# A mixture-of-experts stage put into a hand-written order on every engine

## The chip, the cores and the metric

The kernel runs on one core of a Trainium2 chip. The metric is the device time of one execution in microseconds (us). A core has a matrix engine (TensorE, PE in the rows; PEld is its loading of stationary operands), a vector engine (VectorE, DVE), a scalar engine (ScalarE, ACT), a general engine (GpSimd, POOL) and a queue that issues transfers (SyncE, SP). Each engine works through its own instructions in a fixed order and waits at semaphores for the others.

## The reference, cut to what matters

One transformer block for 256 tokens of width 2048, all in fp32: attention and a gated recurrence, then a hierarchical mixture of experts, on which the change works. A router gives every token one of 4 groups and two of its 8 experts. Cut to the experts:

```python
y = jnp.zeros_like(h)
for gi in range(N_GROUPS):                       # 4 groups of 8 experts
    cg = jnp.where(grp == gi, comb, 0.0)         # weights of the token's two experts
    lo, hi = gi * EXPERTS_PER_GROUP, (gi + 1) * EXPERTS_PER_GROUP
    a = jnp.einsum('bsd,edf->bsef', h, w_gate[lo:hi])
    u = jnp.einsum('bsd,edf->bsef', h, w_up[lo:hi])
    y = y + jnp.einsum('bsef,efd->bsd', jax.nn.silu(a) * u * cg[..., None], w_down[lo:hi])
x = x + gt2[:, None] * y
return rmsnorm(x, g_final)
```

Each of the 32 experts has three matrices of 2048 x 512, 12 MB in fp32; all 32 are read once.

## The kernel before, in words

A framework traces the program and assigns buffers and semaphores; a planner in it, with a cost model of its own, then picks the order in which the instructions of each engine are issued. The order of the text is a starting point that the planner may leave.

The dense stages (input products, attention, recurrence, output product) come first; `route` works out for each token its place among the tokens of each expert (`self.pos`, at most 64 places, `CAP`). Then `experts` (line 1130) goes over the experts in groups of 2, 2 and then seven times 4 (`GATHERS`), and in each group over pairs of experts:

- **Places and gather.** Two matrices of zeros and ones `P` (line 1149, DVE) say which token sits at which place of the group's experts. `gather` (lines 1269 to 1283) multiplies the normalized tokens, held as two rounded halves, by `P`: for each of 16 slices of 128 columns four matmuls (line 1278) into one PSUM bank and one ACTIVATE (line 1281) that writes the slice `xg[j]`. A group's 16 slices are needed by all of its experts; `xg` has 18 buffers.
- **Gate and up.** An expert is worked off in four blocks `u`. A block has two loads of 1 MB (`slot`, lines 1119 to 1125, issued by SP) and multiplies four slices by both (line 1167: 8 fp32 products, which are 16 matmul instructions); gate goes to PSUM partitions 0 to 63, up to 64 to 127.
- **Hidden.** DVE copies the accumulators (line 1170), PE transposes them (line 1173), ACT applies silu (line 1176), DVE multiplies (line 1178).
- **Weights of the places.** For each pair DVE builds weighted places `Pc` (line 1184), PE transposes them (line 1186); from this come the scatter matrix `sc` (line 1188) and a column of token weights `cw` (line 1191).
- **Down and scatter.** Four chunks of 512 columns per pair. Each has two loads of 1 MB, 16 matmul instructions for both experts (line 1201), a scaling by DVE (line 1204), and a split into two rounded halves, the first by ACT (line 1206), the second by DVE (line 1207). `scatter` (lines 1285 to 1294) multiplies both halves by `sc` (four matmuls, line 1291) and DVE adds the two results to the tokens (line 1292). In the text a chunk's scatter stands after the next chunk's split (`waiting`); the planner may place it elsewhere.

All loads of the stage are issued by SP in one queue. Their buffers are a ring of 12 slots of 1 MB in a fixed rotation (`ring_order`: four of "ring", one of "t8", seven of "ring2"), so a load is issued when the matmuls that last read its slot are done. A pair takes 24 loads, the stage 384. PSUM has 4 banks for accumulators (`acc`) and 3 for gather, transposes and scatter (`misc`). Before the last pair's down chunks `prepare_finish` (lines 1305 to 1316) takes two slots of "ring" for the output and restarts the rotation with the two that are left and "ring2". `overflow` runs only if an expert has more than 64 tokens, `finish` scales the result and writes it.

Of the kernel before, what the change touches and what calls it, by code (L numbers as in the profile page):

```python
# [10 lines left out]
OP = mybir.AluOpType  # L11
# [124 lines left out]
class Block:  # L136
# [993 lines left out]
    def experts(self):  # L1130
        self.sec = "moe"
        nc, a = self.nc, self.a
        V = nc.vector
        mm = nc.tensor.matmul
# [3 lines left out]
        gt2 = self.gt2  # L1138
        iota = self.k[:, K_IOTA:K_IOTA + CAP]
        wg, wu, wd = a["w_exp_gate"], a["w_exp_up"], a["w_exp_down"]  # L1140
        waiting = None
        for g4, ge in enumerate(GATHERS):
            first = sum(GATHERS[:g4])
            P = []
            for t in range(2):
                p = self.mt([128, ge, CAP], "P", 4, F32R)
                for i in range(ge):
                    e = first + i
                    V.tensor_scalar(p[:, i, :], iota, self.pos[:, t, e:e + 1], None, op0=OP.is_equal)
                P.append(p.rearrange("p e s -> p (e s)"))  # L1150
            xg = []
            if g4:
                self.gather(P, xg, KT)
            for pr in range(ge // 2):
                e0 = first + 2 * pr
                gT = []
                for i in range(2):
                    e = e0 + i
                    sl = slice((2 * pr + i) * CAP, (2 * pr + i + 1) * CAP)
                    gu = self.acc()  # L1160
                    for u in range(4):
                        wgu = [self.slot(w[e, u], [128, 4, FF]) for w in (wg, wu)]
                        self.gather(P, xg, 4 * u + 4)
                        for jj in range(4):
                            j = 4 * u + jj
                            for k in range(2):
                                mm(gu[64 * k:64 * k + 64, :], xg[j][:, sl], wgu[k][:, jj, :], start=j == 0, stop=j == KT - 1,  # L1167
                                   skip_group_check=True)
                    gs = self.mt([128, FF], "gu", 2)
                    V.tensor_copy(gs, gu)  # L1170
                    ps = self.misc()
                    for f in range(4):
                        nc.tensor.transpose(ps[:, f * 128:(f + 1) * 128], gs[:, f * 128:(f + 1) * 128], self.ident)  # L1173
                    v = ps.rearrange("p (f s) -> p f s", f=4)
                    si = self.mt([128, 4, CAP], "si", 2)
                    nc.scalar.activation(si, v[:, :, 0:CAP], AF.Silu)  # L1176
                    h = self.mt([128, 4, CAP], "hT", 4)
                    V.tensor_mul(h, si, v[:, :, CAP:2 * CAP])
                    gT.append(h)
                ps = self.misc()  # L1180
                for t in range(2):
                    p = self.mt([128, 2, CAP], "Pc", 4)
                    for i in range(2):
                        V.tensor_scalar(p[:, i, :], iota, self.pos[:, t, e0 + i:e0 + i + 1], self.comb[:, t, e0 + i:e0 + i + 1],
                                        op0=OP.is_equal, op1=OP.mult)
                    nc.tensor.transpose(ps[:, t * 128:(t + 1) * 128], p.rearrange("p e s -> p (e s)"), self.ident)
                sc = self.mt([128, 256], "S", 2, F32R)
                V.tensor_scalar(sc, ps[:, 0:256], 0.0, None, op0=OP.is_gt)
                scr = self.mt([128, 256], "Sw", 2)
                cw = self.mt([128, 1], "cw", 2)  # L1190
                nc.scalar.activation(scr, ps[:, 0:256], AF.Copy, accum_out=cw)
                if e0 == N_EXP - 2:
                    self.prepare_finish()
                last = e0 == N_EXP - 2
                for c0, n in LAST_CHUNKS if last else DOWN_CHUNKS:
                    s = slice(c0, c0 + n)
                    wdd = [self.slot(wd[e0 + i, c0 // 512, :, :, c0 % 512:c0 % 512 + n], [128, 4, n]) for i in range(2)]
                    yp = self.acc()
                    for f in range(4):
                        for i in range(2):  # L1200
                            mm(yp[64 * i:64 * i + 64, :n], gT[i][:, f, :], wdd[i][:, f, :], start=f == 0, stop=f == 3,  # L1201
                               skip_group_check=True)
                    raw = self.mt([128, n], "ys", 2)
                    V.scalar_tensor_tensor(raw, yp[:, :n], cw, gt2[:, s], op0=OP.mult, op1=OP.mult)  # L1204
                    ys = [self.mt([128, n], "yp", 4, F32R) for _ in range(2)]
                    nc.scalar.activation(ys[0], raw, AF.Copy)  # L1206
                    V.tensor_sub(ys[1], raw, ys[0].bitcast(F32))
# [3 lines left out]
                if last:  # L1211
                    self.scatter(*waiting)
# [157 lines left out]
```

## Time and profile before

| | before |
|---|---|
| three runs, median (lowest to highest) | 1863.23 us (1863.08 to 1867.92) |
| the profiled execution, and its span from the first to the last instruction | 1862.79 us, 1861.0 us |
| PE busy | 1699.1 us (91% of the span) |
| DVE, ACT busy | 908.2 us (49%), 507.0 us (27%) |
| bytes moved | 630.38 MB, mean 339 GB/s |
| experts' stage, from the first gate matmul to the last instruction | 858.9 to 1861.0 us |

The profile is one execution. The busy time of an engine is the union of its instructions; a PE matmul's end is modelled, so a stretch of matmuls is best read from the start of the first to the start of what follows. The chain of work that ended last, which the profile follows back from the last instruction, ends here within the closing normalization and says nothing about the experts; where the stage is held up has to be read from the waits, the timeline and the stretches.

### The profile page before, as it was taken

Reading aid. Unit: us, or ns where it says so; the run is one execution under the profiler, and the core shown is the slowest. Engines: PE = TensorE matmul, PEld = TensorE weight load, DVE = VectorE, ACT = ScalarE, POOL = GpSimd, SP = SyncE. Lnnn points to the kernel's source line nnn. Section 1 sums busy time; section 2 is a strip of 40 time slices with the busy share of each in tenths; the row PEclk is TensorE's granted clock in tenths of the full one; section 3 lists DMA queues with packets and bytes.
Section 4 is the critical chain, followed back from the end, with each engine's and each line's share of the span. In section 5 each row is a group of like instructions: output and inputs, shape, how many; then the busy total and the mean of one; then the engine's idle time right before and its main releaser. Section 6 shows DMA issues by size and latency. Waiting matters only on the chain. (4 is left out here: it accounts for less than half of the span.)

```text
span 1861.0 us, 20334 instructions
## 1 busy us (share of the span) xinstructions
PE 1699.1 (91%) x7925; PEld 960.1 (52%) x7925; DVE 908.2 (49%) x1636; ACT 507.0 (27%) x845; POOL 17.3 (1%) x36
## 2 busy tenths in 40 slices
PE   6899999999999999997999888898898889988995
PEld 4566676777778878874434343342342423423322
DVE  3677589698788899854221232222212322122124
ACT  3333354555454434433202020020010200201112
POOL 0000000000000000000000000000000000000000
PEclk9999999999999999997999999999999999999998
DMA  7887745776668988868999999999999999999975
GB/s 283 285 292 287 280 163 194 260 290 262 226 246 309 355 310 329 331 226 323 396 400 378 422 421 408 421 394 421 421 393 421 392 422 421 393 420 422 394 311 227
DMA packets 96484, 630.38 MB, mean 339 GB/s; under 512 B 14864, under 2 KB 17216, under 8 KB 22016
## 3 DMA queue, kind: packets, MB, share of 16 engines
q1 hardware_dynamic: 95008, 626.01, 84.6%
q0 software_dynamic: 1200, 2.96, 0.6%
q8 instruction: 64, 1.05, 0.2%
q14 instruction: 36, 0.29, 0.0%
q10 hardware_dynamic: 176, 0.07, 0.0%
HBM read 626.90 MB, written 2.10 MB: 338 GB/s over the span
## 5 line engine op out<-in xcount | busy, mean ns | idle before, releaser
L1167 PE MATMUL moe_acc<-moe_u,moe_xg 128*64 128x512 f32 x2048 | 465.4, 596 | 0.0
L1167 PEld LDWEIGHTS moe_acc<-moe_u,moe_xg 128*64 128x64 f32 x2048 | 148.8, 137 | 285.7 <-issue 280.1
L1201 PE MATMUL moe_acc<-moe_u,moe_hT 128*64 128x512 f32 (+1 forms) x1040 | 261.4, 610 | 0.6 <-DMA moe_u<-w_exp_down 0.6
L1170 DVE COPY moe_gu<-moe_acc 128x512 f32<-128x512 f32 x32 | 22.1, 691 | 409.5 <-PE moe_acc L1167 409.5
L1291 PE MATMUL moe_ps<-moe_yp,moe_S 128*128 128x512 f32 (+1 forms) x260 | 92.5, 440 | 77.1 <-ACT moe_yp L1206 70.0
L1201 PEld LDWEIGHTS moe_acc<-moe_u,moe_hT 128*64 128x64 f32 x1040 | 76.2, 140 | 140.2 <-issue 137.0
L1176 ACT ACTIVATE moe_si<-moe_ps 128x256 f32<-128x256 f32 x32 | 12.3, 384 | 451.8 <-PE moe_ps L1173 451.8
L1204 DVE SCALAR_TENSOR_TENSOR moe_ys<-moe_acc,moe_cw,out_t 128x512 f32<-128x512 f32 (+1 forms) x65 | 48.2, 742 | 171.4 <-PE moe_acc L1201 171.4
L1206 ACT ACTIVATE moe_yp<-moe_ys 128x512 fp32r<-128x512 f32 (+1 forms) x65 | 40.4, 622 | 313.0 <-DVE moe_ys L1204 313.0
L1291 PEld LDWEIGHTS moe_ps<-moe_yp,moe_S 128*128 128x128 f32 x260 | 38.9, 188 | 142.8 <-ACT moe_yp L1206 111.4
L276 PE MATMUL gate_acc<-gate_wr,first_t 128*128 128x512 f32 x256 | 103.3, 404 | 0.0
L277 PE MATMUL gate_acc<-gate_wl,first_t 128*128 128x512 f32 x256 | 102.2, 399 | 0.0
L278 PE MATMUL gate_acc<-gate_wr,first_t 128*128 128x512 f32 x256 | 101.8, 397 | 0.0
L1292 DVE TENSOR_TENSOR out_t<-out_t,moe_ps 128x512 f32<-128x512 f32 (+1 forms) x130 | 83.6, 675 | 31.8 <-PE moe_ps L1291 31.8
L254 ACT ACTIVATE gate_wr<-gate_u 128x1024 fp32r<-128x1024 f32 x64 | 67.8, 1060 | 85.9 <-PE gate_acc L278 80.7
L1281 ACT ACTIVATE moe_xg<-moe_ps,pre_c,pre_c 128x256 f32<-128x256 f32 (+1 forms) x144 | 69.7, 541 | 73.9 <-PE moe_ps L1278 73.8
L255 DVE TENSOR_TENSOR gate_wl<-gate_u,gate_wr 128x1024 fp32r<-128x1024 f32 x64 | 78.0, 1222 | 23.1 <-ACT gate_wr L254 22.7
L1278 PEld LDWEIGHTS moe_ps<-moe_P,out_t 128*128 128x128 f32 x576 | 73.0, 195 | 22.5 <-issue 9.6
L1278 PE MATMUL moe_ps<-moe_P,out_t 128*128 128x256 f32 (+1 forms) x576 | 79.1, 289 | 4.1 <-DVE out_t L1292 3.4
L276 PE MATMUL lb_acc<-lb_wr,first_t 128*128 128x512 f32 (+1 forms) x208 | 78.8, 383 | 3.0 <-ACT first_t L523 2.4
L277 PE MATMUL lb_acc<-lb_wl,first_t 128*128 128x512 f32 (+1 forms) x208 | 78.7, 378 | 2.7 <-DVE lb_wl L255 2.7
L278 PE MATMUL lb_acc<-lb_wr,first_t 128*128 128x512 f32 (+1 forms) x208 | 78.0, 377 | 0.0
(436 smaller groups left out, 2506.5 us busy)
## 6 DMA issues: line engine op xcount, KB each, us to landing
moe_u<-w_exp_gate SPq DMA_DIRECT2D x128, 1024.0 KB, 11.4
moe_u<-w_exp_up SPq DMA_DIRECT2D x128, 1024.0 KB, 13.1
moe_u<-w_exp_down SPq DMA_DIRECT2D x126, 1024.0 KB, 12.3
gate_u<-w_in SPq DMA_DIRECT2D x32, 1024.0 KB, 4.8
gate_u<-w_ada SPq DMA_DIRECT2D x26, 1024.0 KB, 5.7
lb_u<-w_in SPq DMA_DIRECT2D x20, 1024.0 KB, 6.3
first_u<-w_ada SPq DMA_DIRECT2D x17, 1024.0 KB, 5.9
out_u<-w_out SPq DMA_DIRECT2D x16, 1024.0 KB, 6.5
```

The lines of the kernel that those rows point to most:

```text
L254: nc.scalar.activation(hi, raw, AF.Copy)
L255: nc.vector.tensor_sub(lo, raw, hi.bitcast(F32))
L276: mm(out, lr, hi, start=start, stop=False)
L277: mm(out, lr, lo, start=False, stop=False)
L278: mm(out, ll, hi, start=False, stop=stop)
L1167: mm(gu[64 * k:64 * k + 64, :], xg[j][:, sl], wgu[k][:, jj, :], start=j == 0, stop=j == KT - 1, skip_group_check=True)
L1201: mm(yp[64 * i:64 * i + 64, :n], gT[i][:, f, :], wdd[i][:, f, :], start=f == 0, stop=f == 3, skip_group_check=True)
L1204: V.scalar_tensor_tensor(raw, yp[:, :n], cw, gt2[:, s], op0=OP.mult, op1=OP.mult)
L1278: nc.tensor.matmul(ps[:, 0:n], self.xs[t][i][:, j * 128:(j + 1) * 128], P[t], start=t == 0 and i == 0, stop=t == 1 and i == 1)
L1281: nc.scalar.activation(x, ps[:, 0:n], AF.Identity, scale=self.mod["sc2"][:, j:j + 1], bias=self.mod["sh2"][:, j:j + 1])
L1291: self.nc.tensor.matmul(ps[:, :n], sc[:, t * 128:(t + 1) * 128], ys[i], start=i == 0, stop=i == 1)
L1292: self.nc.vector.tensor_add(self.z[t][:, s], self.z[t][:, s], ps[:, :n])
```

## The change

`experts` is rewritten inside `tc.manual_schedule()`: there each engine issues its instructions in the order of the text. That order is new: the first block of the next pair stands before the down chunks; a chunk is scattered after the next chunk's down matmuls, and the last chunk of a pair after block 1 of the next pair; the places of the next group are built, and its gather is issued four slices at a time, between the blocks of the group's last expert; the transposes of an expert's first member stand after the first block of its second. What is computed stays, and so do the loads, tile sizes, buffers and ring. The removed loop is printed above; "..." stands for removed lines, and blank lines are left out.

```diff
@@ -1128,90 +1128,150 @@
         return self.moe.tile(shape, dt, name=self.name(tag), tag=tag, bufs=bufs)
     def experts(self):
         self.sec = "moe"
         nc, a = self.nc, self.a
...
         self.ring_i = 0
         self.ring_order = [("ring", self.big)] * 4 + [("t8", self.big)] * 1 + [("ring2", self.moe)] * R2
         self.z = self.x2
...
+        self.we = wg, wu, wd = a["w_exp_gate"], a["w_exp_up"], a["w_exp_down"]
+        group = []
+        for g, n in enumerate(GATHERS):
+            group += [(g, i) for i in range(n)]
+        P, xg = {}, {}
+        gu, hT = {}, {}
+        def places(g):
+            P[g] = self.places(sum(GATHERS[:g]), GATHERS[g])
+            xg[g] = []
+        def block(e, u):
+            g, i = group[e]
+            if u == 0:
+                gu[e] = self.acc()
+            w = [self.slot(w[e, u], [128, 4, FF]) for w in (wg, wu)]
+            if g == 0:
+                self.gather(P[g], xg[g], 4 * u + 4)
+            for jj in range(4):
+                j = 4 * u + jj
+                for k in range(2):
+                    nc.tensor.matmul(gu[e][64 * k:64 * k + 64, :], xg[g][j][:, CAP * i:CAP * i + CAP], w[k][:, jj, :],
+                                     start=j == 0, stop=j == KT - 1, skip_group_check=True)
+        last = N_EXP - 2
         waiting = None
...
+        with self.tc.manual_schedule():
+            places(0)
+            for e0 in range(0, N_EXP, 2):
+                e1 = e0 + 1
+                g, i = group[e1]
+                more = i == GATHERS[g] - 1 and g + 1 < len(GATHERS)
+                for u in range(1 if e0 else 0, 4):
+                    block(e0, u)
+                    if u == 1 and waiting:
+                        self.scatter(*waiting)
+                        waiting = None
+                gs = self.products_out(gu.pop(e0))
+                if more:
+                    places(g + 1)
+                for u in range(4):
+                    block(e1, u)
+                    if u == 0:
+                        hT[e0] = self.hidden(gs)
+                        Pc = self.weighted_places(e0)
+                    if more and u < 3:
+                        self.gather(P[g + 1], xg[g + 1], 4 * u + 4)
+                gs = self.products_out(gu.pop(e1))
+                sc, cw = self.turned_places(Pc)
+                if more:
+                    self.gather(P[g + 1], xg[g + 1], KT)
+                hT[e1] = self.hidden(gs)
+                if e0 == last:
                     self.prepare_finish()
...
+                else:
+                    block(e0 + 2, 0)
+                h = hT.pop(e0), hT.pop(e1)
+                for c0, n in LAST_CHUNKS if e0 == last else DOWN_CHUNKS:
+                    ys = self.down(h, cw, e0, c0, n)
                     if waiting:
                         self.scatter(*waiting)
                     waiting = (sc, ys, c0, n, e0)
...
+            self.scatter(*waiting)
+        self.overflow(wg, wu, wd, self.gt2)
         self.finish()
+    def places(self, first, n):
+        iota = self.k[:, K_IOTA:K_IOTA + CAP]
+        P = []
+        for t in range(2):
+            p = self.mt([128, n, CAP], "P", 4, F32R)
+            for i in range(n):
+                e = first + i
+                self.nc.vector.tensor_scalar(p[:, i, :], iota, self.pos[:, t, e:e + 1], None, op0=OP.is_equal)
+            P.append(p.rearrange("p e s -> p (e s)"))
+        return P
+    def products_out(self, gu):
+        gs = self.mt([128, FF], "gu", 2)
+        self.nc.vector.tensor_copy(gs, gu)
+        return gs
+    def hidden(self, gs):
+        nc = self.nc
+        ps = self.misc()
+        for f in range(4):
+            nc.tensor.transpose(ps[:, f * 128:(f + 1) * 128], gs[:, f * 128:(f + 1) * 128], self.ident)
+        v = ps.rearrange("p (f s) -> p f s", f=4)
+        si = self.mt([128, 4, CAP], "si", 2)
+        nc.scalar.activation(si, v[:, :, 0:CAP], AF.Silu)
+        h = self.mt([128, 4, CAP], "hT", 4)
+        nc.vector.tensor_mul(h, si, v[:, :, CAP:2 * CAP])
+        return h
+    def weighted_places(self, e0):
+        iota = self.k[:, K_IOTA:K_IOTA + CAP]
+        Pc = []
+        for t in range(2):
+            p = self.mt([128, 2, CAP], "Pc", 4)
+            for i in range(2):
+                self.nc.vector.tensor_scalar(p[:, i, :], iota, self.pos[:, t, e0 + i:e0 + i + 1],
+                                             self.comb[:, t, e0 + i:e0 + i + 1], op0=OP.is_equal, op1=OP.mult)
+            Pc.append(p)
+        return Pc
+    def turned_places(self, Pc):
+        nc = self.nc
+        ps = self.misc()
+        for t in range(2):
+            nc.tensor.transpose(ps[:, t * 128:(t + 1) * 128], Pc[t].rearrange("p e s -> p (e s)"), self.ident)
+        sc = self.mt([128, 256], "S", 2, F32R)
+        nc.vector.tensor_scalar(sc, ps[:, 0:256], 0.0, None, op0=OP.is_gt)
+        scr = self.mt([128, 256], "Sw", 2)
+        cw = self.mt([128, 1], "cw", 2)
+        nc.scalar.activation(scr, ps[:, 0:256], AF.Copy, accum_out=cw)
+        return sc, cw
+    def down(self, h, cw, e0, c0, n):
+        nc = self.nc
+        wd = self.we[2]
+        w = [self.slot(wd[e0 + i, c0 // 512, :, :, c0 % 512:c0 % 512 + n], [128, 4, n]) for i in range(2)]
+        yp = self.acc()
+        for f in range(4):
+            for i in range(2):
+                nc.tensor.matmul(yp[64 * i:64 * i + 64, :n], h[i][:, f, :], w[i][:, f, :], start=f == 0, stop=f == 3,
+                                 skip_group_check=True)
+        raw = self.mt([128, n], "ys", 2)
+        nc.vector.scalar_tensor_tensor(raw, yp[:, :n], cw, self.gt2[:, c0:c0 + n], op0=OP.mult, op1=OP.mult)
+        ys = [self.mt([128, n], "yp", 4, F32R) for _ in range(2)]
+        nc.scalar.activation(ys[0], raw, AF.Copy)
+        nc.vector.tensor_sub(ys[1], raw, ys[0].bitcast(F32))
+        return ys
     def overflow(self, wg, wu, wd, gt2):
```

## Rows read from the trace of the kernel before

**Rows 1.** The page's 40 slices of the span: what the transfers moved.

```profile
GB/s 283 285 292 287 280 163 194 260 290 262 226 246 309 355 310 329 331 226 323 396 400 378 422 421 408 421 394 421 421 393 421 392 422 421 393 420 422 394 311 227
```

**Rows 2.** Stretches: length, each engine's busy time (instructions), clock, DMA share, GB/s.

```profile
1010.00:1095.00 85.00, 74.01 (x328) 25.34 (x326) 22.68 (x41) 5.88 (x13) 0.00 (x0) 1.00 1.01 421
1100.00:1120.00 20.00, 19.57 (x112) 11.66 (x113) 4.60 (x13) 8.37 (x17) 0.00 (x0) 1.00 0.96 389
864.80:1844.60 979.80, 876.95 (x4055) 342.36 (x4055) 242.38 (x473) 134.57 (x289) 0.00 (x0) 0.99 0.97 399
```

**Rows 3.** Waits of the SP queue from 700 us: total, times, longest.

```profile
SPq L1122 <- PE moe_acc L1167: 443.6, 237, 20.2
SPq L1122 <- PE moe_acc L1201: 354.6, 119, 7.1
```

**Rows 4.** Groups by line from 800 us: busy, mean ns, idle before, its releaser.

```profile
L1167 PE MATMUL moe_acc<-moe_u,moe_xg 128*64 128x512 f32 x2048 | 465.4, 596 | 0.0
L1201 PE MATMUL moe_acc<-moe_u,moe_hT 128*64 128x512 f32 (+1 forms) x1040 | 261.4, 610 | 0.6 <-DMA moe_u<-w_exp_down 0.6
L1291 PE MATMUL moe_ps<-moe_yp,moe_S 128*128 128x512 f32 (+1 forms) x260 | 92.5, 440 | 77.1 <-ACT moe_yp L1206 70.0 <-DVE moe_hT L1178 7.1
L1173 PE MATMUL moe_ps<-pre_c,moe_gu 128*128 128x128 f32 x128 | 21.0, 286 | 22.5 <-DVE moe_gu L1170 22.5
```

**Rows 5.** Timeline of one down chunk: start, duration, what runs, idle before it.

```profile
1770.97 0.75 DVE L1204 SCALAR_TENSOR_TENSOR moe_ys<-moe_acc,moe_cw,out_t 128x512 f32<-128x512 f32 x1 [2.53 <-PE moe_acc L1201]
1771.76 0.63 ACT L1206 ACTIVATE moe_yp<-moe_ys 128x512 fp32r<-128x512 f32 x1 [5.92 <-DVE moe_ys L1204]
1772.42 0.69 DVE L1207 TENSOR_TENSOR moe_yp<-moe_ys,moe_yp 128x512 fp32r<-128x512 f32 x1 [0.70 <-ACT moe_yp L1206]
...
1772.44 1.46 PE L1291 MATMUL moe_ps<-moe_yp,moe_S 128*128 128x512 f32 x4 [1.50 <-ACT moe_yp L1206]
...
1773.71 1.28 DVE L1292 TENSOR_TENSOR out_t<-out_t,moe_ps 128x512 f32<-128x512 f32 x2 [0.59 <-PE moe_ps L1291]
...
1773.84 3.65 PE L1201 MATMUL moe_acc<-moe_u,moe_hT 128*64 128x512 f32 x16
```

**Rows 6.** Timeline of PE: a gather's stretch, an expert's blocks, transposes, a slow chunk.

```profile
1109.27 5.05 PE L1278 MATMUL moe_ps<-moe_P,out_t 128*128 128x256 f32 x40
1114.26 13.95 PE L1167 MATMUL moe_acc<-moe_u,moe_xg 128*64 128x512 f32 x64
1128.99 0.66 PE L1173 MATMUL moe_ps<-pre_c,moe_gu 128*128 128x128 f32 x4 [0.78 <-DVE moe_gu L1170]
...
1153.42 5.35 PE L1201 MATMUL moe_acc<-moe_u,moe_hT 128*64 128x512 f32 x16
```

**Rows 7.** Timeline at the stage's start.

```profile
807.25 0.33 SPq L1122 DMA_DIRECT2D moe_u<-w_exp_gate  x1
...
854.81 0.73 DVE L1149 TENSOR_SCALAR moe_P<-pre_c,route_c 128x64 fp32r<-128x64 f32 x4
...
864.80 0.33 SPq L1122 DMA_DIRECT2D moe_u<-w_exp_gate  x1
```

**Rows 8.** Timeline at the stage's end.

```profile
1790.98 0.33 SPq L1122 DMA_DIRECT2D moe_u<-w_exp_up  x1
...
1813.87 3.26 SPq L1122 DMA_DIRECT2D moe_u<-w_exp_down  x6
...
1842.70 1.94 PE L1201 MATMUL moe_acc<-moe_u,moe_hT 128*64 128x256 f32 x14
```

**Rows 9.** Stretches of 2 us at the stage's end.

```profile
1802.00:1804.00 2.00, 2.00 (x10) 0.56 (x6) 0.00 (x0) 0.77 (x2) 0.00 (x0) 1.00 0.14 57
...
1814.00:1816.00 2.00, 2.00 (x12) 0.72 (x10) 0.00 (x0) 0.00 (x0) 0.00 (x0) 1.00 0.49 127
...
1836.00:1838.00 2.00, 2.00 (x12) 0.70 (x10) 1.75 (x5) 1.35 (x4) 0.00 (x0) 1.00 0.24 74
```

**Rows 10.** The stretch of the slow chunk of Rows 6.

```profile
1153.00:1157.00 4.00, 4.00 (x12) 1.19 (x13) 1.28 (x2) 0.00 (x0) 0.00 (x0) 0.57 1.02 424
```

More of the change, by code (lines that the diff above doesn't have):

```diff
@@ L1132, in experts @@
         nc, a = self.nc, self.a
-        V = nc.vector
-        mm = nc.tensor.matmul
         self.ring_i = 0
@@ L1137, in experts @@
         self.z = self.x2
-        gt2 = self.gt2
-        iota = self.k[:, K_IOTA:K_IOTA + CAP]
-        wg, wu, wd = a["w_exp_gate"], a["w_exp_up"], a["w_exp_down"]
-        waiting = None
[L1142 to L1192, printed above, removed]
-                    self.prepare_finish()
[L1194 to L1207, printed above, removed]
@@ L1210, in experts @@
                     waiting = (sc, ys, c0, n, e0)
-                if last:
-                    self.scatter(*waiting)
-        self.overflow(wg, wu, wd, gt2)
+            self.scatter(*waiting)
+        self.overflow(wg, wu, wd, self.gt2)
         self.finish()
+    def places(self, first, n):
[8 more added lines that the diff above has]
+        return P
```

## The prediction

> **What bounds the kernel now.** I read the page's slices first, because the experts' stage is a stream of weights: 384 loads of 1 MB (1.0486 MB). From slice 21 on most slices move 420 to 423 GB/s, and every third or fourth falls to about 393 [rows 1]. The stretches show the same twice: 421 GB/s over 85 us without a gather, with PE busy for 74.01 of them, and 389 GB/s over 20 us with one, with PE busy for 19.57 [rows 2]. So the transfers have a ceiling, 421 GB/s, or 1.0486 / 0.421 = 2.491 us for a load and 24 x 2.491 = 59.8 us for a pair of experts. They don't stay at it: from the first refill of the ring to the last down matmul the mean is 399 GB/s [rows 2].
>
> The SP queue's waits say who holds the stream back. SP waits 443.6 + 354.6 us for matmuls to free a slot [rows 3], while the down matmuls wait 0.6 us in all for data and the gate matmuls not at all [rows 4]. Today PE sets the pace and the transfers follow close behind. The pace is 979.8 / 16 = 61.2 us for a pair, of which PE is busy 876.95 / 16 = 54.8 [rows 2]. Most of the difference stands in two groups: 77.1 us idle before the scatter's matmuls, nearly all for ACT's rounded half, and 22.5 us before the transposes of the hidden products [rows 4], together 99.6 / 16 = 6.2 us for a pair. The timeline shows the first: a chunk is scattered directly behind its own down matmuls, so PE stands 1.50 us while DVE scales (0.75) and ACT rounds (0.63) [rows 5], although the text has the scatter one chunk later.
>
> So there are two limits close together, 61.2 us by PE as it is ordered now and 59.8 us by the transfers. What the change is worth is the distance to the second, plus what the ends of the stage give.
>
> **The change, part by part.**
>
> *Scatter behind the next chunk's down matmuls.* From the start of the scaling to the end of the second half's subtraction a chunk takes 1773.11 - 1770.97 = 2.1 us, and the next down matmuls, which now lie in between, 3.65 [rows 5]. That covers the wait with 1.5 us to spare; the last chunk of a pair is covered by a block, 13.95 / 4 = 3.5 us [rows 6]. If the cover were gone, the wait would return at 1.5 us a chunk, 6.0 a pair. In the fixed order DVE's subtraction waits 0.70 us for ACT with the previous chunk's two additions queued behind it; DVE's chunk is 0.75 + 0.70 + 0.69 + 1.28 = 3.4 us against 3.65 + 1.46 = 5.1 on PE [rows 5], so the additions free their PSUM banks in time.
>
> *Transposes.* The first expert's wait of 0.78 us [rows 6] is covered by the block of 3.5 us now ahead of it. The second expert has only the turned places ahead (two transposes; about half of 0.66, 0.3, as an estimate), so some 0.4 us a pair stays, and block 0 of the next pair is queued behind it. That block covers silu and product.
>
> *Gather.* The same matmuls, 5.05 / 40 = 0.126 us each [rows 6], 64 for four experts: 8.1 us, 4.0 a pair. In one piece they are 8.1 us in which no slot comes free. Spread over four blocks they are 2.0 us a piece, less than what PE will spend waiting for a load (below). The order also respects `xg`: 18 buffers leave two beyond a group's 16, and each block frees four ahead of the four slices it is followed by. The places of the next group go to DVE, which is busy 22.68 of 85 us [rows 2]; nothing waits for them before the gather.
>
> *PE's new pair:* blocks 2 x 13.95 = 27.9, down 4 x 3.65 = 14.6, scatters 4 x 1.46 = 5.8, transposes 2 x 0.66 + 0.3 = 1.6, gather 4.0, wait 0.4: 54.3 us, with 54.8 from the busy time as a check. That is 5 us under the transfers' 59.8, so the bound changes over from PE to the loads. Of the 6.2 us of waits taken away only 1.4 can come off the pace; the rest becomes waiting for loads.
>
> *SP's queue* still issues in the order of use (block 0 of the next pair moves ahead of the down loads on SP as on PE), so nothing in it blocks something that is needed sooner. With 12 slots, of which PE holds two, a full ring has ten loads or 25 us on order, and a stall of PE shorter than that stops no transfer.
>
> **The sum,** made on the profiled execution (1862.79 us; the median of the three runs is 1863.2).
> - The first 12 loads are issued from 807.25 on, and the first refill goes out at 864.80, when block 0 is done [rows 7]; neither depends on the new order. Bytes start to flow about 1.5 us after an issue (1813.87; 127 GB/s in 1814 to 1816 is 0.25 MB, or 0.6 us at the ceiling, so from 1815.4) [rows 8, 9].
> - During the first pair PE carries the gathers of the first two groups and frees slots a little slower than the loads come (16 gather matmuls at 0.126 and a block, 5.5 us, against 4.98 for two loads), so I add 4 us for gaps.
> - Loads 13 to 376, the last gate and up block: 364 x 2.491 = 906.7 us. The last lands at 864.8 + 1.5 + 4 + 906.7 = 1777.0. Before, it landed at 1802.3 (57 GB/s in 1802 to 1804 is 0.3 us at the ceiling) [rows 9].
> - 376 is 31 rotations of 12 and 4, so the last four gate and up loads sit in the four "ring" slots; two of these go to the output, and the first down load must wait for the last block, 3.5 us: 1780.5. From the first down load's issue to the last byte it takes 22.5 us, as before (1813.87 to 1836.4) [rows 8, 9]: 1803.0. `prepare_finish` now stands on PE between the last transposes and the first down matmuls, in a time in which these wait for loads anyway.
> - After the last byte, the last half chunk's matmuls: 1.9 us, and from their end to the end of the span 1861.0 - 1844.64 = 16.4 us [rows 8], with 0.6 for DVE's order (the third chunk's additions now stand behind the last split): 1803.0 + 18.9 = 1821.9.
> - Span to time, 1.8 us: 1823.7. **I predict 1824 us,** 39 us or 2.1% less: about 25 from the stream, 8 from a shorter gap before the last down loads (13.1 us without bytes before, 5.0 after), 6 because PE no longer trails the last byte by 8.2 us.
>
> The Trainium skill ("DMA: Bandwidth & Descriptors", Specifications) puts the ceiling of a core's transfers into its memory at 435 GB/s. By it a load would be 2.41 us and the end some 29 us earlier. The rows stay at 421 with the queue full, so I don't use it.
>
> **The rivals.**
> 1. *The waits stay on PE* (0.09). If the halves are late after all, because DVE or ACT are held up in the fixed order, the scatter's wait comes back. At 1.5 us a chunk PE's pair is 54.3 + 6.0 = 60.3 and the stage gains 16 x 0.9 = 14 us: 1849. Against it: 1.5 us of spare cover for each chunk.
> 2. *The first loads are held* (0.07). If the fixed part starts only when routing is done (the first places are built at 854.81 [rows 7]), the ring is empty then: 854.8 + 1.5 + 376 x 2.491 = 1792.9 in place of 1777.0, so 1840. For it: I can't see how the planner joins the two parts. Against it: SP's queue has nothing in it that waits for routing.
> 3. *No change* (0.05). The transfers are already at their ceiling in most slices; if they and not PE set the end, removing waits on PE gives nothing: 1863. Against it: PE never waits for data, SP always for PE.
> 4. *Slower, by the clock* (0.07). With loads as the bound PE works 3.5 us of every 4.98 in the blocks and stands 1.5. After idle times of that length the clock does fall now: five times in the stage a stretch like 1153 to 1157 has a granted clock of 0.57, that is partly 1.2 GHz, behind stalls of 1.5 us, and the chunk in it takes 5.35 us in place of 3.65 [rows 6, 10], 1.7 more. If it fell in each of the 8 blocks of a pair, a pair would be 54.3 + 13.6 = 67.9 us, 6.7 over today's: 1863 + 107 = 1970. It decides against the change from (61.2 - 54.3) / 1.7 = 4 falls a pair. Against it: PE stands only if the loads are behind, and a slow block then eats waiting time, not time of the stream; the lead of up to ten loads takes up 1.7 us many times over. The Trainium skill has this rule ("TensorE: Matmul & The Clock Gate", HAM oscillation): a kernel whose matmuls between two load waits are short drops to the low clock again at every wait. The trace agrees only in part, five falls at 65 scatters (260 matmuls, four each [rows 4]).
>
> **How the numbers follow.** My own case has 0.72. Its bounds: 1819 if the last down loads needn't wait for the last block (5 us less), 1834 if new waits of the fixed order and more gaps in the first pairs cost 10 us; a little lower if the queue, always full, runs somewhat faster than 421. With rival 2 and half of rival 1 the range 1812 to 1848 holds 0.83. Faster by over 0.3% (5.6 us, about what a measurement of this kernel can tell from no change): 0.72 + 0.09 + 0.07 = 0.88; within it 0.05; slower 0.07.
>
> **What would show it.** Right: the slices of the stage at about 421 throughout, without the dips at the gathers; the gate and down matmuls waiting for loads, 4 to 5 us a pair in the later pairs; SP's waits for PE shorter than the loads' queue; no idle time before the scatter's matmuls; the first down load of the last pair within 4 us of the last block's data. Wrong: dips that stay; idle time before the scatter for ACT or DVE; first loads issued after 845; a granted clock below 0.9 over the stage; or transfers that with a full queue move less than 415.

## The result, and the profile after

The changed kernel takes 1834.12 us (median of 4 runs, 1830.15 to 1837.2) against 1865.58 us (4 runs, 1863.08 to 1868.08) for the kernel before on the same chip: ratio 0.983 [0.9801, 0.9859], 31 us less. The forecast was 1824 in 1812 to 1848. The profiled execution took 1836.52 us, its span is 1834.8 us, 26.2 less than before. One run of one experiment (the other end, without GpSimd) took 2426.03 us at a mean granted clock of 0.65 and stays out of that experiment's numbers.

First the page's slices of the changed kernel: the granted clock and what the transfers moved, to be held against [rows 1].

```profile
PEclk9999999999999999997999999999999999999997
GB/s 284 292 286 282 288 158 205 250 293 250 230 232 327 335 310 318 348 261 265 379 422 421 421 421 422 421 421 421 421 422 421 421 421 422 421 421 421 422 377 192
```

The dips at the gathers are gone: from slice 21 to slice 38 the transfers stay at 420 to 422 GB/s. Next the waits of the SP queue (total, times, longest), which answer to [rows 3], and the groups by line that answer to [rows 4].

```profile
SPq L1122 <- DMA moe_u<-w_exp_gate: 229.2, 104, 12.0
SPq L1122 <- DMA moe_u<-w_exp_down: 212.0, 104, 2.1
SPq L1122 <- DMA moe_u<-w_exp_up: 210.3, 102, 2.1
SPq L1122 <- PE moe_acc L1160: 118.2, 69, 19.5
SPq L1122 <- PE moe_acc L1267: 28.6, 23, 3.9
```

```profile
L1160 PE MATMUL moe_acc<-moe_u,moe_xg 128*64 128x512 f32 x2048 | 487.6, 600 | 42.1 <-DMA moe_u<-w_exp_up 42.1
L1267 PE MATMUL moe_acc<-moe_u,moe_hT 128*64 128x512 f32 (+1 forms) x1040 | 242.1, 590 | 10.9 <-DMA moe_u<-w_exp_down 10.9
...
L1351 PE MATMUL moe_ps<-moe_yp,moe_S 128*128 128x512 f32 (+1 forms) x260 | 78.4, 422 | 2.6 <-ACT moe_yp L1272 2.3 <-DVE out_t L1352 0.2
...
L1227 PE MATMUL moe_ps<-pre_c,moe_gu 128*128 128x128 f32 x128 | 20.6, 283 | 3.4 <-DVE moe_gu L1219 3.4
```

The two waits have changed places. Before, SP waited 798 us for PE and PE waited for no load; now SP waits 147 us for PE, and the gate and down matmuls (lines 1160 and 1267) stand 53 us for loads. The scatter's wait fell from 77.1 to 2.6 us, that of the transposes from 22.5 to 3.4. The timeline of PE shows a chunk and a block, to compare with [rows 5, 6].

```profile
974.09 1.20 PE L1351 MATMUL moe_ps<-moe_yp,moe_S 128*128 128x512 f32 x4
975.22 3.65 PE L1267 MATMUL moe_acc<-moe_u,moe_hT 128*64 128x512 f32 x16
978.80 1.21 PE L1351 MATMUL moe_ps<-moe_yp,moe_S 128*128 128x512 f32 x4
...
1050.62 3.65 PE L1160 MATMUL moe_acc<-moe_u,moe_xg 128*64 128x512 f32 x14 [1.32 <-DMA moe_u<-w_exp_up]
```

A chunk takes 978.80 - 974.09 = 4.71 us. From 1020 on blocks stand 1.3 us for a load, where the prediction had 1.5. Now the stretches (columns as in [rows 2]): 750 us of the stage, then the end, as in [rows 9].

```profile
1025.00:1775.00 750.00, 695.56 (x3116) 292.03 (x3115) 186.22 (x363) 93.81 (x196) 0.00 (x0) 1.00 1.01 421
...
1776.00:1778.00 2.00, 2.00 (x13) 0.89 (x10) 0.40 (x2) 0.00 (x0) 0.00 (x0) 1.00 0.75 315
1778.00:1780.00 2.00, 1.07 (x6) 0.19 (x2) 0.00 (x0) 0.00 (x0) 0.00 (x0) 1.00 0.57 238
1780.00:1782.00 2.00, 1.71 (x8) 0.63 (x10) 0.00 (x0) 0.00 (x0) 0.00 (x0) 1.00 0.43 180
1782.00:1784.00 2.00, 1.94 (x10) 0.56 (x6) 0.00 (x0) 0.00 (x0) 0.00 (x0) 1.00 0.19 78
...
1792.00:1794.00 2.00, 1.88 (x3) 0.87 (x4) 0.76 (x4) 0.00 (x0) 0.00 (x0) 0.58 1.05 442
1794.00:1796.00 2.00, 2.00 (x3) 0.71 (x3) 1.16 (x6) 0.95 (x4) 0.00 (x0) 0.56 0.97 410
...
1804.00:1806.00 2.00, 2.00 (x10) 0.76 (x8) 0.75 (x1) 0.23 (x1) 0.00 (x0) 1.00 0.88 276
1806.00:1808.00 2.00, 2.00 (x10) 0.69 (x12) 1.57 (x3) 0.58 (x2) 0.00 (x0) 1.00 0.03 12
```

In the middle the rate is the ceiling and the clock 1.00. Only the end is untidy: the rate falls over 8 us before the last down loads start, and the last bytes move at about 1806.1. The timeline of the end shows what PE does then, to compare with [rows 8].

```profile
1783.13 3.19 SPq L1122 DMA_DIRECT2D moe_u<-w_exp_down  x6
...
1789.66 0.66 PE L1227 MATMUL moe_ps<-pre_c,moe_gu 128*128 128x128 f32 x4 [0.41 <-DVE moe_gu L1219]
1791.11 1.65 DVE L1360 TENSOR_SCALAR moe_ys<-pre_c,lb_c 128x128 f32<-128x128 f32 x8
1792.12 5.71 PE L1362 MATMUL moe_acc<-moe_ys,pre_c 128*128 128x512 f32 x8 [1.80 <-DVE moe_ys L1360]
1797.76 7.09 PE L1267 MATMUL moe_acc<-moe_u,moe_hT 128*64 128x512 f32 x32
...
1813.65 1.95 PE L1267 MATMUL moe_acc<-moe_u,moe_hT 128*64 128x256 f32 x16
1818.15 0.48 DVE L1270 SCALAR_TENSOR_TENSOR moe_ys<-moe_acc,moe_cw,out_t 128x256 f32<-128x256 f32 x1
```

The closing rows of `prepare_finish` (line 1362: the factors of the output's scaling, built by DVE and multiplied out by PE) wait 1.80 us for DVE and then run 5.71 us at a granted clock of 0.56 to 0.58, partly the lower of its two levels. The first down matmul starts at 1797.76, with its loads there: it waits for none. The last one ends at 1815.6, 9.5 us behind the last byte.

### The profile page after: what moved, and what is told of

Same layout as the page of the kernel before. It is cut to its first block, busy times and chain, and to the rows that moved or that the text cites. A ratio compares the mean times of both kernels' runs of the same rounds, so it can differ in the third digit from the quotient of the medians.

```text
span 1834.8 us, 20408 instructions
## 1 busy us (share of the span) xinstructions
PE 1713.7 (93%) x7925; PEld 992.0 (54%) x7925; DVE 903.0 (49%) x1636; ACT 505.5 (28%) x845; POOL 17.2 (1%) x36
## 5 line engine op out<-in xcount | busy, mean ns | idle before, releaser
L1160 PE MATMUL moe_acc<-moe_u,moe_xg 128*64 128x512 f32 x2048 | 487.6, 600 | 42.1 <-DMA moe_u<-w_exp_up 42.1
L1160 PEld LDWEIGHTS moe_acc<-moe_u,moe_xg 128*64 128x64 f32 x2048 | 157.3, 137 | 319.1 <-issue 219.0
L1267 PE MATMUL moe_acc<-moe_u,moe_hT 128*64 128x512 f32 (+1 forms) x1040 | 242.1, 590 | 10.9 <-DMA moe_u<-w_exp_down 10.9
L1267 PEld LDWEIGHTS moe_acc<-moe_u,moe_hT 128*64 128x64 f32 x1040 | 88.3, 137 | 145.9 <-issue 109.5
L1338 PEld LDWEIGHTS moe_ps<-moe_P,out_t 128*128 128x128 f32 x576 | 72.7, 194 | 22.0 <-issue 16.1
L1351 PE MATMUL moe_ps<-moe_yp,moe_S 128*128 128x512 f32 (+1 forms) x260 | 78.4, 422 | 2.6 <-ACT moe_yp L1272 2.3
L278 PE MATMUL lb_acc<-lb_wr,first_t 128*128 128x512 f32 (+1 forms) x208 | 78.4, 378 | 0.0
L1351 PEld LDWEIGHTS moe_ps<-moe_yp,moe_S 128*128 128x128 f32 x260 | 44.0, 189 | 60.3 <-issue 49.9
## 6 DMA issues: line engine op xcount, KB each, us to landing
moe_u<-w_exp_gate SPq DMA_DIRECT2D x128, 1024.0 KB, 19.8
moe_u<-w_exp_up SPq DMA_DIRECT2D x128, 1024.0 KB, 19.8
moe_u<-w_exp_down SPq DMA_DIRECT2D x126, 1024.0 KB, 19.8
```

The lines of the kernel that those rows point to most:

```text
L278: mm(out, ll, hi, start=False, stop=stop)
L1160: nc.tensor.matmul(gu[e][64 * k:64 * k + 64, :], xg[g][j][:, CAP * i:CAP * i + CAP], w[k][:, jj, :], start=j == 0, stop=j == KT - 1, skip_ ...
L1267: nc.tensor.matmul(yp[64 * i:64 * i + 64, :n], h[i][:, f, :], w[i][:, f, :], start=f == 0, stop=f == 3, skip_group_check=True)
L1338: nc.tensor.matmul(ps[:, 0:n], self.xs[t][i][:, j * 128:(j + 1) * 128], P[t], start=t == 0 and i == 0, stop=t == 1 and i == 1)
L1351: self.nc.tensor.matmul(ps[:, :n], sc[:, t * 128:(t + 1) * 128], ys[i], start=i == 0, stop=i == 1)
```

## The experiments

Each was run beside the kernel before on the same chip, with 4 runs of each experiment and 7 of before. The medians of before: 1867.37 us for the first four below, 1865.14 us for the cover, the fewer loads and the last two, 1865.43 us for the control and the first three edits of the end. Runs of one kernel lie up to 10 us apart, and the changed kernel's own two medians, 1834.12 and the control's 1837.48, differ by 3.4 us, so that much between two medians can't be told from none.

**The old text in fixed order.** The loop of before, unaltered, under the fixed order:

```diff
+        with self.tc.manual_schedule():
             for g4, ge in enumerate(GATHERS):
...
```

> The kernel before with its own text, but issued in the order of that text. There each scatter already stands behind the next chunk's down matmuls; the other waits stay in (two transposes of 0.8 us, some 2 us before the first down chunk, about 1 us for the places of a group), so PE's pair is 54.3 + 4 to 5 = 58 to 59 us. If the place of the scatter is what counts and the loads (59.8 us a pair) are the new bound, nearly the whole gain comes: 1832 to 1842. If the pipeline (next pair's block first, gather spread) is needed for it, less than half of the gain: above 1850.

Measured: 1855.94 us, ratio 0.9949 [0.9933, 0.9966]: a third of the gain, so the place of the scatter isn't all that counts. The scatter's wait is gone here too, since the old text already had the scatter a chunk behind (2.5 us in all). Two fences show what is left: PE's timeline around the first gather, and a stretch of it.

```profile
920.26 1.21 PE L1292 MATMUL moe_ps<-moe_yp,moe_S 128*128 128x512 f32 x4
924.18 12.46 PE L1279 MATMUL moe_ps<-moe_P,out_t 128*128 128x128 f32 x64 [2.71 <-DVE moe_P L1150]
936.57 15.48 PE L1168 MATMUL moe_acc<-moe_u,moe_xg 128*64 128x512 f32 x64
```

```profile
920.00:940.00 20.00, 17.29 (x80) 14.06 (x80) 3.29 (x8) 7.93 (x17) 0.00 (x0) 0.66 0.50 209
```

The places stand right ahead of their gather, so PE waits 2.71 us for DVE, the clock falls to 0.66, and the gather takes 12.46 us, during which no slot comes free: 209 GB/s. From 880 to 1020 this kernel moves 7.0 MB less than the changed one (7 stretches of 20 us, mean 362 against 411 GB/s), which is 16.6 us at 421. From 1020 on it too stays at 421 GB/s, and the same wait (3.04 us at 1351.90, the gather then 9.84) costs the stream nothing there.

**The new text, order left to the planner.** The reverse:

```diff
-        with self.tc.manual_schedule():
+        if True:
```

> The changed kernel with its new text, but with the planner's order. In the program's order the scatter now stands behind its own chunk's down matmuls and one more matmul (0.43 us of cover). If the place of the scatter counts, about 1.1 us of wait a chunk comes back, PE's pair is near 59 to 60 and the time 1838 to 1852. If the new text is what counts, as fast as the changed kernel, 1830 to 1837.

Measured: 1908.46 us, ratio 1.0238 [1.0213, 1.0263], slower than before and than either expectation. The group of the scatter and SP's first wait:

```profile
L1351 PE MATMUL moe_ps<-moe_yp,moe_S 128*128 128x512 f32 (+1 forms) x260 | 93.8, 448 | 91.6 <-ACT moe_yp L1272 91.5
```

```profile
SPq L1122 <- PE moe_acc L1160: 560.3, 247, 20.5
```

PE waits 1.56 us for ACT ahead of a scatter again (at 1300.63 and 1307.24): the planner puts it behind its own chunk's down matmuls. The text alone gains nothing, then; it is the order.

**The scatter behind its own chunk**, in the fixed order:

```diff
-                    if u == 1 and waiting:
-                        self.scatter(*waiting)
-                        waiting = None
...
-                    if waiting:
-                        self.scatter(*waiting)
-                    waiting = (sc, ys, c0, n, e0)
-            self.scatter(*waiting)
+                    self.scatter(sc, ys, c0, n, e0)
```

> The changed kernel with each scatter directly behind its own chunk's down matmuls, all else as changed. By the sum PE's pair becomes 54.3 + 4 x 1.5 = 60.3 or a little more, over the loads' 59.8, and SP waits for PE again: 1846 to 1856, with 1.5 us of idle time before each scatter. If the loads alone set the end, 1834 with the waits taken from the waits for loads.

Measured: 1890.59 us, ratio 1.0138 [1.0114, 1.0161]: 56 us more than the changed kernel, and more than the expectation allowed. The same group and SP's first two waits:

```profile
L1345 PE MATMUL moe_ps<-moe_yp,moe_S 128*128 128x512 f32 (+1 forms) x260 | 95.6, 449 | 117.7 <-ACT moe_yp L1266 103.4 <-DVE moe_yp L1267 14.1
```

```profile
SPq L1122 <- PE moe_acc L1160: 449.3, 108, 19.7
SPq L1122 <- PE moe_acc L1261: 312.0, 60, 7.7
```

Idle and busy together the scatter costs (117.7 - 2.6 + 95.6 - 78.4) / 65 = 2.0 us a chunk more than when deferred, not the 1.5 that I took from one chunk's wait; in the kernel before, by [rows 4], it was (77.1 - 2.6 + 92.5 - 78.4) / 65 = 1.4. At 8 us a pair PE is the bound again, and SP waits 761 us for it. Of the parts tried, this is the one that the change can't do without; the old text in fixed order, which has it too, shows that it isn't enough by itself.

**The gather in one piece**, after the turned places:

```diff
-                    if more and u < 3:
-                        self.gather(P[g + 1], xg[g + 1], 4 * u + 4)
```

> The changed kernel with a group's gather in one piece of 8.1 us at the end of the last expert's blocks. If a full ring (ten loads, 25 us) carries the stream over it, no change: within 3 us of the changed kernel's 1834, slices still at 421 GB/s. If the spreading is what removed the dips, they come back at seven gathers, some 1 to 2 us each: 1841 to 1848.

Measured: 1833.95 us, ratio 0.9825 [0.9809, 0.9841], as the changed kernel. The page's slices:

```profile
GB/s 281 288 286 284 282 172 206 258 294 244 232 232 330 334 310 325 342 257 259 389 423 421 421 421 421 421 421 421 421 421 421 421 421 421 421 421 421 421 384 193
```

There are no dips, so spreading the gather is worth nothing that can be measured: with its places built early, the loads on order carry it.

**No cover for the transposes**: the hidden products directly behind their copy, the next pair's block 0 after the down chunks.

```diff
-                for u in range(1 if e0 else 0, 4):
+                for u in range(4):
...
+                hT[e0] = self.hidden(gs)
...
-                        hT[e0] = self.hidden(gs)
...
-                else:
-                    block(e0 + 2, 0)
```

> The changed kernel without the cover of its transposes: the first expert's hidden products directly behind their copy, and block 0 of the next pair no longer ahead of the down chunks. The scatter's deferral and the spread gather stay. The waits before the transposes should come back, some 0.8 + 0.8 us and 1.4 for the places, about 3 us a pair on PE. Theory (loads set the pace): PE's pair is then still under 59.8, so 1834 to 1842. Rival (these waits are what kept the text of before, put in fixed order, at 1856): 1850 to 1858.

Measured: 1833.36 us, ratio 0.9841 [0.9811, 0.987], as the changed kernel. The groups of the gate matmuls and of the transposes:

```profile
L1160 PE MATMUL moe_acc<-moe_u,moe_xg 128*64 128x512 f32 x2048 | 484.6, 600 | 30.6 <-DMA moe_u<-w_exp_up 30.3
...
L1225 PE MATMUL moe_ps<-pre_c,moe_gu 128*128 128x128 f32 x128 | 20.6, 283 | 16.1 <-DVE moe_gu L1217 16.1
```

The transposes wait 16.1 us again (3.4 in the changed kernel), and the waits for loads fall from 53.0 to 31.9 us (30.3, and 1.6 at the down matmuls). A wait of PE only takes the place of a wait for a load. So the covers of transposes and block 0 are, by themselves, not what separates the old text from the new; what remains is that there the places stand right ahead of their gather, and the gather at the start of a group. That is by elimination and not shown: the places alone were not moved, and the covers and the spread gather were not taken away together.

**Fewer loads**, to see what sets the pace. In 15 pairs the chunk at column 1536 uses the first expert's down weights for both experts, so 23 loads of 24 are left.

```diff
+        w = [self.slot(...) for i in range(1 if c0 == 1536 and n == 512 else 2)]
+        w = (w * 2)[:2]
```

> The changed kernel with one load less for a pair: in the chunk at column 1536 of 15 pairs the first expert's down weights are used for both experts, so the second expert's are not read there; everything else, all matmuls included, stays. Theory (in the changed kernel the loads set the pace of most pairs, 24 x 2.49 = 59.8 us against 53 to 57 of PE): 23 loads take 57.3 us; the three or so first pairs, which PE paces, give little, so about 12 x 2.49 = 30 us less: 1800 to 1812. Rival (PE or the fixed order sets the pace, and the waits for loads only show where its slack stands): within 5 us of the changed kernel, 1830 to 1838.

Measured: 1797.3 us, ratio 0.9645 [0.9616, 0.9674], below the 1800 to 1812 expected. That is 36.8 us less than the changed kernel in its first runs and 40.2 less than in the control below, which ran on the same chip; 15 x 2.491 = 37.4 would be all of it. The page's slices and the first of SP's waits:

```profile
GB/s 279 286 283 307 274 196 165 258 281 266 218 260 281 355 305 310 347 320 222 332 408 418 421 421 421 421 421 421 422 421 422 421 421 421 420 422 420 422 421 173
```

```profile
SPq L1122 <- DMA moe_u<-w_exp_gate: 209.8, 102, 3.0
```

The same rate, fewer bytes, and the time follows them at the full price as near as the runs can tell, in the first pairs too, where I had expected little: there PE still works off what the ring holds, but the stream behind it is already at its ceiling. Counted from the ninth load, the fourth pair's loads are issued 7.9 us earlier than in the changed kernel, and three loads are 7.5 us. The loads set the pace of the changed kernel.

**The end of the stage.** A control and three edits: the closing rows put behind the last expert's four blocks; the output's two ring slots taken before the last pair's loads, with the rotation kept; and both.

```diff
+                    if e0 == last:
+                        self.finish_row(u)
...
+                    if e0 + 2 == last:
+                        self.take_output()
```

> The changed kernel itself, to be compared with the three beside it: 1830 to 1837.

> The changed kernel with the four rows of the closing scale (16 small DVE operations, four matmuls, eight copies, which stand between the last transposes and the first down matmuls) spread behind the four blocks of the last expert. If these rows are what makes PE trail the last loads (first down matmuls 7.4 us after the last transposes, the second of them at half clock), the end comes 5 to 10 us earlier: 1824 to 1830. If the end is set by the landing of the last down loads, no change against the kernel beside it.

> The changed kernel with the two ring slots for the output taken before the last pair's blocks and the rotation kept, so that the first down loads of the last pair don't wait for its last blocks. The stream then has no gap (some 6 us are lost there now). If the closing rows set the end, 0 to 4 us less than the kernel beside it; if the last loads set it, 5 to 7 us less.

> Both edits. If the rows trail the loads and the gap delays the loads, the two add up here, where neither hides the other: 10 to 14 us less than the changed kernel, 1819 to 1825.

Measured: control 1837.48 us (ratio 0.9845 [0.9819, 0.9872]), rows early 1838.24 (0.9855 [0.9831, 0.9879]), ring early 1834.49 (0.9837 [0.9811, 0.9862]), both 1834.08 (0.9836 [0.9807, 0.9865]). None is told from the control, and the 1819 to 1825 hoped for from both was missed. With the ring taken early the rate no longer falls ahead of the last down loads; two stretches of that run, beside the 238 and 78 GB/s above:

```profile
1778.00:1780.00 2.00, 1.05 (x6) 0.17 (x2) 0.00 (x0) 0.00 (x0) 0.00 (x0) 1.00 1.01 422
...
1782.00:1784.00 2.00, 1.98 (x10) 0.56 (x6) 0.00 (x0) 0.00 (x0) 0.00 (x0) 1.00 1.04 434
```

But PE reaches its first down matmul at 1796.23 all the same. With the rows early the DVE factors come too late, PE stands 2.7 us ahead of the first row, and each row pushes the blocks by 1.1 us.

So I rebuilt the end once more: each row's DVE part one block ahead of its matmuls, the rows spread over both experts of the last pair, the ring early, a chunk's closing scaling one chunk later; then the same with half of that scaling on GpSimd.

```diff
+                    if e0 == last and u > 1:
+                        self.finish_row(dg, ...)
+                    if e0 == last and u:
+                        dg = self.row_factors(u - 1)
...
-                nc.vector.tensor_mul(self.zg[t][:, b:b + 256], ...)
+                (nc.gpsimd if t else nc.vector).tensor_mul(self.zg[t][:, b:b + 256], ...)
```

> The changed kernel with another end: each of the four closing rows is multiplied out between the blocks of the last pair, its vector part one block earlier; the two ring slots of the output are taken before the last pair's loads; the scaling of a chunk's columns stands one chunk later. Theory (the end trails the last byte by 10 us because of the closing rows, the half clock behind them and the order on DVE): 6 to 9 us less than the changed kernel, 1825 to 1829. Rival (the last pair's down chunks are bound by PE and DVE themselves): as with both partial edits before, 1832 to 1836.

> As the run with the other end before, and the closing scaling of the second half of the tokens is done by GpSimd in place of DVE. If DVE is what ends last, 1 to 3 us less than that run, 1823 to 1828; if GpSimd's multiplications are slow or share a port with DVE, the same or up to 4 us more.

Measured: 1832.11 us (0.9834 [0.9803, 0.9864]) without GpSimd, 1831.78 us (0.9826 [0.9803, 0.9848]) with it. Both miss the time that they were hoped to reach, 1825 to 1829 and 1823 to 1828. PE's timeline at the end of the first:

```profile
1785.26 4.00 PE L1160 MATMUL moe_acc<-moe_u,moe_xg 128*64 128x512 f32 x16
...
1790.63 4.65 PE L1282 MATMUL moe_acc<-moe_u,moe_hT 128*64 128x512 f32 x18
1795.55 3.65 PE L1282 MATMUL moe_acc<-moe_u,moe_hT 128*64 128x512 f32 x14 [0.27 <-DMA moe_u<-w_exp_down]
...
1808.38 1.95 PE L1282 MATMUL moe_acc<-moe_u,moe_hT 128*64 128x256 f32 x16
...
1813.82 1.58 PE L1366 MATMUL moe_ps<-moe_yp,moe_S 128*128 128x256 f32 x4 [2.29 <-ACT moe_yp L1287]
```

In the profiles the edit does what it should: the down matmuls start 7.1 us earlier than 1797.76 and wait for loads again, and from the last block's start to the end it takes 1830.2 - 1785.26 = 44.9 us against 1834.8 - 1785.22 = 49.6. DVE is busy for 11.03 of the 12 us from 1806. Giving half of the scaling to GpSimd relieves it little: the same stretch takes 1827.8 - 1783.44 = 44.4 us, and DVE's two multiplications of a chunk, with GpSimd's two beside them, take 1.28 us, where all four on DVE alone took 1.43. The medians are 2.0 and 2.3 us under the changed kernel's first, which the runs can't tell from none; they are 5.4 and 5.7 under the control's, but that was measured beside other runs. So no version was found that beats the changed kernel for certain.

## Why the prediction was right, and where it was off

- **The bound and the ceiling**: right. PE left the path, the loads took it, at 421 GB/s for 750 us on end; the fewer loads show that the price of a load is 2.45 us (36.8 / 15), or 2.68 against the control, where the sum had 2.491. The Trainium skill ("DMA: Bandwidth & Descriptors", Specifications) has 435 GB/s as the ceiling of the fabric; with the queue never empty the trace stays at 421, so the row and not the page was the right one to sum with.
- **The scatter**: right. The wait is gone (2.6 us of 77.1), so rival 1 is out, and with the gain of 31 us rival 3 (no change); and deferring also gives back some of the matmuls' own time (440 to 422 ns each), which I hadn't counted.
- **The transposes and the gather's spreading**: the stalls went away as described, and I priced them rightly as waits that turn into waits for loads. The experiments show that neither is needed as long as the rest of the new order stays.
- **PE's new pair**: 54.3 us predicted. Where PE still set the pace, the one pair that I read, with a whole gather in it, took 57.2 us (block 0 of the next pair at 927.45 and at 984.67). The sum for such a pair is 54.3 - 4.0 + 8.1 = 58.4, so it was 1.2 too high: a chunk with its scatter takes 4.71 and not 3.65 + 1.46.
- **The gaps of the first pair**: 380 GB/s in 868 to 880, 398 and 373 in 880 to 900 and 900 to 920, (41 x 12 + 23 x 20 + 48 x 20) / 421 = 4.5 us, against the 4 assumed.
- **The first refill** came at 866.06 instead of 864.80; the delay is older than the stage, whose first load was 2.0 us late already (809.23 against 807.25). Rival 2 is out.
- **The last down loads**: issued at 1783.13, 2.6 us later than the 1780.5 of the sum, and not for its reason. The wait of 3.5 us for the last block didn't come: the issue lies before that block's start at 1785.22, as in the kernel before (1813.87, and the last block from 1814.52), so the sum had misread it. SP waited until 1777.8 for a load to land and then 5.3 us for gate matmuls, those of the block before, which started at 1780.29. By this working it is late by the fall of the rate ahead of it, (421 x 4 - 315 - 238 - 180 - 78) x 2 us = 1.75 MB or 4.1 us, and by the late start of 1.3. From this issue to the last byte it took 23.0 us (22.5 in the sum).
- **The step that failed in its size** is the sentence that `prepare_finish` stands "in a time in which these wait for loads anyway". The last pair's down work takes PE 1815.6 - 1797.76 = 17.8 us, so it had to start by 1790.2 to end 1.9 us behind the last byte. The rows held it until 1797.76. I had looked at when the first load would land, not at how long PE's queue behind it is. After the last byte came 28.7 us in place of 18.9: by this working 7.6 from PE's late start, 2.2 from DVE's order (the last half chunk's scaling waits until 1818.15 behind additions and multiplications, where I had put 0.6). The rows are only a part of it: in the other end without GpSimd the down matmuls start at 1790.63, but they end at 1810.3, only 5.3 us earlier, and again 6 us behind the last byte (37 GB/s in 1804 to 1806, so at about 1804.2). The sum took the last byte for what ends last; with the rows or without, it is PE's down work, counted from the last block.
- **The whole**: 1821.9 + 2.6 + 0.5 + 9.8 = 1834.8, the span.
- **Rival 4**, the clock: refuted. Blocks stand 1.3 us for loads again and again, and the clock is 1.00 over the 750 us. The Trainium skill's rule ("TensorE: Matmul & The Clock Gate", HAM oscillation), by which short matmul groups between load waits lose the clock at every wait, doesn't show here; the page's own case has longer waits, so it isn't refuted there. The clock did fall behind 2.71 us in the old text's gather, and behind 1.80 us ahead of the closing rows. But with the ring taken early the same rows waited 1.81 us and ran at 1.00 (1.95 us for four of the eight), so the one wait doesn't decide it.

## What to carry to other kernels

When a wait is removed, work out the next limit first: here 6.2 us a pair of waits could give 1.4, and neither the spread gather nor the covered transposes gave anything on top of it. Which limit holds is shown by taking some of it away: one load in 24 less brought the whole price of the load. A stop of PE costs time only where PE is the one that is late; the old text's wait ahead of a gather cost (421 - 209) x 20 / 421 = 10 us of transfers in one stretch at the start, and none later, when PE waited for the loads. At the end of a stage, count the consumer's whole remaining work back from the last byte, and forward from the last block before it, not only its first wait.

## What was not expected of the hardware

Loads take longer from issue to landing although the rate is at its ceiling. The page's transfers (KB each, median us from issue to landing), before and after:

```profile
moe_u<-w_exp_gate SPq DMA_DIRECT2D x128, 1024.0 KB, 11.4
```

```profile
moe_u<-w_exp_gate SPq DMA_DIRECT2D x128, 1024.0 KB, 19.8
```

19.8 us is 8 x 2.49: no more than eight loads are on their way at once, where I had counted ten, and SP's 651 us of waits for transfers are for the landing of an earlier load and not for a slot. The trace shows what sets the eight: the loads report their landing on eight semaphores in turn, and SP waits, ahead of nearly every issue, for the load eight places earlier on the same semaphore (the load issued at 1762.96 followed a landing at 1762.89). It is the program's limit, then, beside the slots. It costs nothing here, since eight are enough for the ceiling.

The rate falls gradually where the loads on order run out (315, 238, 180, 78 GB/s in 2 us each), while in the kernel before it fell within 2 us [rows 9]. The semaphores show how. A load reports in sixteen parts; those of the last gate and up load come in from 1776.34 to 1785.18, and in the kernel before from 1802.49 to 1804.25. From the first part to the last it takes 5.8 us in the changed kernel (median of the loads on six of the eight semaphores), 1.7 in the kernel before and 1.9 with the scatter behind its own chunk, where PE holds the loads back. So under a queue that never runs empty the parts drift apart, the last one sets the landing, and the rate falls as one part after the other runs out. Why the parts are unequal was not tried.
